# A feed-forward kernel's second product: T1 before the context's B22, the norm's scale row in PSUM, statistics right behind a tile's last part, and B12 before T2 in step one

## The chip, the cores and the metric

The kernel runs on one core of one Trainium2 chip. The metric is the time of one execution in microseconds on the device, as the median of the runs on record.

## What is computed

One layer of a bidirectional hybrid backbone, for 128 context tokens and 1,024 latent tokens of width 1,024. The change touches its last part alone, the second half of the squared-ReLU MLP with its residual and layer norm:

```python
def layer_norm(x, g=None, b=None):
    mu = jnp.mean(xf, -1, keepdims=True)
    var = jnp.mean(jnp.square(xf - mu), -1, keepdims=True)
    y = (xf - mu) * lax.rsqrt(var + LN_EPS)
    y = y * g + b
...
hid = jnp.square(jax.nn.relu(u @ lw['w_fc'] + lw['b_fc']))
x = layer_norm(ALPHA * x + gate2 * (hid @ lw['w_proj'] + lw['b_proj']), lw['ln_g'][1], lw['ln_b'][1])
```

`hid` has 4,096 columns, `w_proj` is 4,096 by 1,024, all in float32; `gate2` is a row of 1,024, one for the context and one for the latents.

## The kernel before

Function `ffn2` computes `hid @ w_proj` in four steps of 1,024 rows of `w_proj` each (`F2`). Every operand is split into a high half, a copy that ScalarE rounds (`hi`, or `w[..., 0]`), and a low half, the rest, subtracted on VectorE or GpSimd (`lo`, `w[..., 1]`; all these have line L68, the copies L67). A product is then three matmuls: high by high, high by low, low by high (`mm3`, lines L111 to L113).

**Products of a step.** The eight weight row blocks of a step come in four pairs; each pair gives the blocks B11, B12 (left and right 512 columns of the first row block), B21 and B22 (of the second). The latents use a seven-product scheme: hidden-layer sums stored in DRAM beforehand (`h_d`) times B11, B21, T2, T3, T4, T1 and B22. T2, T3 and T4 are differences of the blocks that `source` makes just before they are split: VectorE subtracts twice a pair for T2 (L1446, L1447, the second into `tb`), GpSimd once for T3 (L1449) and once for T4 (L1451). T1's block is the first difference of T2, left in place. The 128 context tokens use the four plain blocks with their own hidden layer (`hc_d`). One product for the latents is four blocks `j` of 128 tokens with 12 matmuls of 512 columns each; one for the context is 12 matmuls.

**Order.** `KINDS` (and `KINDS0` in step one) lists the products. For each, `block` runs the four `j`, adds the PSUM bank into the float32 accumulators `C` on VectorE (L1553, L1555), and, for the plain blocks, `context` adds the context's share (L1535). Weights are prepared by a generator, `ahead`, which the loop advances twice a block with `step_work`: it loads raw weights (`load_raw`, L1437) and hidden-layer units (`f2_load`, L1364 and L1367) on SP's queue, and emits splits. At most five half-weights may be prepared ahead of use (`tiles`); they sit in a ring of four buffers and one more. `until` drives the generator until a product's weights have been emitted. All engines run their instructions in the order in which they were emitted, SP's queue of transfers too.

**Ending of step four.** Accumulator tiles are tokens: tile 0 is the context, tiles 1 to 8 are latents, of which 1 to 4 take their right half from B22 and 5 to 8 theirs from T1. `finish` adds the bank to the accumulator, multiplies by the gate and adds the residual with a running sum (L1592, L1593, L1576: three vector operations); `later` does the gate product of tiles 0 to 4's left half on GpSimd (L1585). `norm` is a generator: mean (L1600), ScalarE's Square with its sum (L1601) and root (L1602), then VectorE's reciprocal (L1604); ScalarE's Identity scales and shifts (L1612); the product with the row `lng` and the sum with `lnb` (L1615, L1616) are GpSimd's, or half VectorE's where `how` is 1. Where `how` is 2, VectorE does all in four operations (L1607, L1608). `pump` advances each started norm by one part after each block. B22's context product comes first, then T1's four blocks, then B22's.

Of the kernel before, what the change touches and what calls it, by code (L numbers as in the profile page):

```python
# [12 lines left out]
OP = mybir.AluOpType  # L13
# [26 lines left out]
class Kern:  # L40
# [1306 lines left out]
    KINDS = ["B11", "B12", "B21", "T2", "T3", "T4", "T1", "B22"]  # L1347
    KINDS0 = ["B11", "B21", "T2", "B12", "T3", "T4", "T1", "B22"]
    ROW = {"B11": 0, "T1": 4, "T2": 5, "T3": 2, "B21": 1, "T4": 3, "B22": 6}
# [64 lines left out]
    def ffn2(self, st):  # L1414
# [15 lines left out]
        NB = len(self.F2)  # L1430
        raws = {}

# [5 lines left out]

        def source(b, kind, k):
            f1, f2 = raws[b, k, 0], raws.get((b, k, 1))  # L1440
            b11, b12 = f1[:, 0:512], f1[:, 512:D]
            if kind in ("B11", "B12"):
                return b11 if kind == "B11" else b12
            b21, b22 = f2[:, 0:512], f2[:, 512:D]
            if kind == "T2":
                v.tensor_tensor(b11, b12, b11, OP.subtract)  # L1446
                v.tensor_tensor(t2[k], b22, b11, OP.subtract)  # L1447
            elif kind == "T3":
                g_.tensor_tensor(b12, b22, b12, OP.subtract)  # L1449
            elif kind == "T4":  # L1450
                g_.tensor_tensor(t2[k], b21, t2[k], OP.subtract)  # L1451
            if kind in ("T2", "T4"):
                return t2[k]
            return {"T3": b12, "T1": b11, "B22": b22, "B21": b21}[kind]
# [5 lines left out]
        def ahead():  # L1460

            self.f2_load(0, None)
            for i in range(2):
                load_raw(0, i)
            yield
            for b in range(NB):
# [5 lines left out]
                for kind in self.KINDS if b else self.KINDS0:  # L1472
                    if (b, kind) in done:
                        continue
                    if b == 0 and kind == "T2":
                        for i in range(2):
                            self.f2_split(b, None, i)
                        done.add((b, "ctx"))
# [3 lines left out]
                    if n is not None:  # L1482
                        while 7 * b + n >= 3 and 7 * b + n - 3 not in used:
                            yield
                        self.f2_load(b, n)
                        split += [lambda i=i, n=n: self.f2_split(b, n, i, g_ if i else v) for i in range(2)]
                    for i in range(2):
# [8 lines left out]
                        yield  # L1496
                    done.add((b, kind))

        work = ahead()
# [56 lines left out]

        rows, xh, tails, outs = {}, {}, [], []
        tile_of = lambda t: ctx if t == 0 else Cj[(t - 1) % 4][:, 2 * ((t - 1) // 4):2 * ((t - 1) // 4) + 2].rearrange("p a n -> p (a n)")
        hs = [slice(0, 512), slice(512, D)]
        xq = [(t, n) for ts, n in (((1, 2, 3, 4, 0), 0), ((5, 6, 7, 8), 0), ((0, 5, 6, 7, 8, 1, 2, 3, 4), 1)) for t in ts]  # L1560

# [34 lines left out]
        def norm(t, how=0):  # L1596
# [8 lines left out]
            if how == 2:  # L1605
                for s in hs:
                    v.scalar_tensor_tensor(y[:, s], y[:, s], q(2), rows["lng"][:, s], OP.add, OP.mult)  # L1607
                    v.scalar_tensor_tensor(y[:, s], y[:, s], q(6), rows["lnb"][:, s], OP.mult, OP.add)  # L1608
                    nc.scalar.dma_start(O["y"][t][:, s], y[:, s])
                return  # L1610
            v.tensor_scalar(q(7), q(2), q(6), None, op0=OP.mult)
            nc.scalar.activation(y, y, AF.Identity, scale=q(6), bias=q(7))  # L1612
            yield
            for s, e in zip(hs, (v, g_)) if how else [(slice(0, D), g_)]:
                e.tensor_tensor(y[:, s], y[:, s], rows["lng"][:, s], OP.mult)  # L1615
                e.tensor_tensor(y[:, s], y[:, s], rows["lnb"][:, s], OP.add)  # L1616
            outs.append(lambda: nc.sync.dma_start(O["y"][t], y))

        def pump():
            for x in tails[:]:  # L1620
                if next(x, tails) is tails:
                    tails.remove(x)
            while outs and not xq:
                outs.pop(0)()
# [3 lines left out]
        sb = [big("S") for _ in range(2)]  # L1628
        tails.append(self.store(15, self.H15, [sb[0][:, 0:512], sb[0][:, 512:D], sb[1][:, 0:512]]))
        for b in range(NB):  # L1630
# [4 lines left out]
            for kind in (self.KINDS if b else self.KINDS0)[:6 if last else 8]:  # L1635
                until(b, kind)
                if kind != "B12":
                    for j in range(4):
# [3 lines left out]
                        else:  # L1642
                            block(b, kind, j)
                        if b or kind != "B11":
                            step_work(2)
# [20 lines left out]

        until(b, "B22")
        row("lng", tb[:, 0, 0:D], I["ln_g"][1:2, :])
        row("lnb", tb[:, 1, 0:D], I["ln_b"][1:2, :])
        context(b, "B22", True)  # L1670
        pump()
        finish(0, 1, cx[1])
        tmp, junk = bank("cx", 2), big("junk")
        tails.append(norm(0))
        for j in range(4):
            ps = banks["C", j] = bank()
            product(b, "T1", j, ps, True)
            finish(5 + j, 1, ps, tmp)
            pump()
            tails.append(norm(5 + j))  # L1680
        for j in range(4):
            product(b, "B22", j, banks["C", j], False)
            finish(1 + j, 1, banks["C", j])
            pump()
            tails.append(norm(1 + j, min(j, 2)))
        while tails or outs:
            pump()
# [79 lines left out]
```

## Time and profile before

| | us |
|---|---|
| median of three runs (2229.61 to 2234.83) | 2231.91 |
| profiled execution: time of the run | 2234.51 |
| profiled execution: span | 2232.4 |
| TensorE busy, 12,507 matmuls | 2112.8 (95%) |
| VectorE busy | 1409.6 (63%) |
| ScalarE busy | 994.9 (45%) |
| GpSimd busy | 854.0 (38%) |
| first and last matmul of the second product | 1822.9 and 2203.7 |

PE is TensorE, DVE VectorE, ACT ScalarE, POOL GpSimd; SPq and ACTq are queues of transfers. Matmuls overlap in their pipeline, so a share of 95% says that TensorE rarely stands, not that it runs at its peak. A busy share is a mean over stages of different limits: what counts in one stage is read from windows of that stage. The mean granted clock of TensorE over the span is 0.981 of 2.4 GHz.

### The profile page before, as it was taken

The numbers are of one execution on the slowest core, as the hardware profiler recorded it, in microseconds if no ns is written. First come the engines' busy times: TensorE is split into PE (matmuls) and PEld (weight loads), VectorE is DVE, ScalarE is ACT, GpSimd is POOL, SyncE is SP. The second block draws the span as 40 slices with busy tenths as digits, with TensorE's granted clock in tenths as the row PEclk, the third lists the DMA queues.
The fourth block names the chain that finished last, engine by engine and source line by source line (L and its number), as shares of the span: only waits on it lengthen the run. The fifth ranks groups of instructions, "written<-read, shape, count | busy, mean of one in ns | idle before, by whom it ended". The sixth has DMA issues, their size and how long they took to land. (4 is left out here: it accounts for less than half of the span.)

```text
span 2232.4 us, 31968 instructions
## 1 busy us (share of the span) xinstructions
PE 2112.8 (95%) x12507; PEld 1986.1 (89%) x12507; DVE 1409.6 (63%) x2248; ACT 994.9 (45%) x1634; POOL 854.0 (38%) x507
## 2 busy tenths in 40 slices
PE   7999999999999999999989999999999998999984
PEld 3889999999999989999989998899999996888863
DVE  4456776676675644888564656866454556566677
ACT  5455425414424525777721423655444443343333
POOL 1402213312421312332212214448566656466476
PEclk9999999999999999999989999999999999999997
DMA  7121241142122141110533333454343464342532
GB/s 275 38 71 50 66 146 64 54 133 86 62 87 83 53 77 46 48 48 29 165 120 128 118 117 115 131 199 136 125 143 121 147 245 158 136 170 79 204 118 108
DMA packets 116647, 251.13 MB, mean 112 GB/s; under 512 B 21332, under 2 KB 53716, under 8 KB 111888
## 3 DMA queue, kind: packets, MB, share of 16 engines
q1 hardware_dynamic: 94976, 231.19, 30.7%
q10 hardware_dynamic: 21520, 17.90, 2.4%
q8 instruction: 98, 1.61, 0.3%
q14 instruction: 53, 0.43, 0.1%
HBM read 186.38 MB, written 62.67 MB: 112 GB/s over the span
## 5 line engine op out<-in xcount | busy, mean ns | idle before, releaser
L111 PE MATMUL pj<-hi,w 128*128 128x384 f32 (+1 forms) x2144 | 712.8, 332 | 18.1 <-ACT XP L805 7.9
L112 PE MATMUL pj<-lo,w 128*128 128x384 f32 (+1 forms) x2144 | 709.8, 331 | 12.9 <-DVE lo L68 6.3
L113 PE MATMUL pj<-hi,w 128*128 128x384 f32 (+1 forms) x2144 | 709.2, 331 | 1.3 <-POOL w L68 1.1
L111 PEld LDWEIGHTS pj<-hi,w 128*128 128x128 f32 x2144 | 406.4, 190 | 20.3 <-ACT XP L805 8.2
L112 PEld LDWEIGHTS pj<-lo,w 128*128 128x128 f32 x2144 | 406.4, 190 | 15.4 <-DVE lo L68 6.9
L113 PEld LDWEIGHTS pj<-hi,w 128*128 128x128 f32 x2144 | 406.0, 189 | 1.9 <-POOL w L68 1.4
L68 POOL TENSOR_TENSOR w<-ws,w 128x512 fp32r<-128x512 f32 (+1 forms) x64 | 113.1, 1769 | 292.0 <-ACT w L67 283.8
L111 PE MATMUL pps<-w,hi 128*128 128x512 f32 x512 | 204.0, 398 | 11.3 <-ACT w L67 9.1
L112 PE MATMUL pps<-w,hi 128*128 128x512 f32 x512 | 204.0, 398 | 6.2 <-POOL w L68 4.1
L113 PE MATMUL pps<-w,lo 128*128 128x512 f32 x512 | 202.9, 396 | 1.4 <-DVE lo L68 1.4
L68 DVE TENSOR_TENSOR w<-ws,w 128x1024 fp32r<-128x1024 f32 (+1 forms) x85 | 112.7, 1334 | 122.6 <-ACT w L67 122.5
L67 ACT ACTIVATE w<-ws 128x1024 fp32r<-128x1024 f32 (+1 forms) x149 | 129.5, 878 | 80.8 <-PE pj L113 67.5
L467 POOL PARTITION_ALL_REDUCE aacc<-aacc x16 | 56.0, 3541 | 256.6 <-DVE aacc L466 256.6
L722 POOL TENSOR_TENSOR CS<-Cst,CS 128x516 fp32r<-128x516 f32 x56 | 73.8, 1319 | 158.2 <-ACT CS L721 147.7
L111 PE MATMUL pj<-Th,w 128*128 128x288 f32 x416 | 123.3, 296 | 8.0 <-ACT e L1297 8.0
L111 PEld LDWEIGHTS pps<-w,hi 128*128 128x128 f32 x512 | 98.0, 191 | 34.5 <-ACT w L67 10.4
L112 PEld LDWEIGHTS pps<-w,hi 128*128 128x128 f32 x512 | 98.0, 191 | 29.7 <-POOL w L68 4.9
L113 PE MATMUL pj<-Th,w 128*128 128x288 f32 x416 | 122.6, 295 | 0.0
L112 PE MATMUL pj<-Tl,w 128*128 128x288 f32 x416 | 122.5, 295 | 0.0
L113 PEld LDWEIGHTS pps<-w,lo 128*128 128x128 f32 x512 | 98.1, 192 | 23.4 <-DVE lo L68 1.9
L68 POOL TENSOR_TENSOR lo<-lo,hi 128x1024 fp32r<-128x1024 f32 (+1 forms) x31 | 84.8, 2735 | 74.0 <-ACT hi L67 74.0
L67 ACT ACTIVATE w<-raw 128x512 fp32r<-128x512 f32 x88 | 50.9, 622 | 109.9 <-issue 62.8
(348 smaller groups left out, 4493.2 us busy)
## 6 DMA issues: line engine op xcount, KB each, us to landing
ws<-in_w_in SPq DMA_DIRECT2D x56, 512.0 KB
lo<-h_d SPq DMA_DIRECT2D x28, 1024.0 KB
aw<-in_w_ada SPq DMA_DIRECT2D x64, 256.0 KB
ws<-in_w_fc SPq DMA_DIRECT2D x32, 512.0 KB
h_d<-Hf SPq DMA_DIRECT2D x32, 512.0 KB
raw<-in_w_pr SPq DMA_DIRECT2D x32, 512.0 KB
h_d<-S SPq DMA_DIRECT2D x48, 256.0 KB
gm<-gs ACTq DMA_DIRECT2D x48, 192.0 KB
```

Of the source, the lines that this page charges most:

```text
L67: self.nc.scalar.activation(hi, x, AF.Copy)
L68: (eng or self.nc.vector).tensor_tensor(lo, x, hi.bitcast(F), OP.subtract)
L111: mm(out, lhsT=ah, rhs=bh, start=first, stop=False, skip_group_check=onto)
L112: mm(out, lhsT=ah, rhs=bl, start=False, stop=False, skip_group_check=onto)
L113: mm(out, lhsT=al, rhs=bh, start=False, stop=last, skip_group_check=onto)
L467: nc.gpsimd.partition_all_reduce(acc[j], acc[j], channels=128, reduce_op=ReduceOp.add)
L722: nc.gpsimd.tensor_tensor(CS[d][1], Cst[d], CS[d][0].bitcast(F), OP.subtract)
```

## The change

- In the last step T1's four blocks come before the context's B22, and each is followed by that tile's mean, Square and root at once (`start`) and by two steps of the weight generator. The residual loads are reordered to match.
- The norm's scale row is copied into two PSUM banks (`lng`), and VectorE's intermediate result `u` lies in PSUM too, so that each of its scaling operations has one large operand there. The context's norm is VectorE's (`how` 2), tiles 2 and 3 are halved between GpSimd and VectorE. VectorE's tiles are stored by SP's queue, no longer ScalarE's.
- In steps two to four T2's and T3's subtractions are emitted right behind B12's and B21's weights (`raw_done`).
- In step one B12 comes before T2, T2's hidden-layer unit is loaded ahead of the second row blocks' weights, these are loaded in halves, the right ones first, and the sums of the last hidden rows (`last_sums`) start after T3's first block instead of at once.

```diff
-    KINDS0 = ["B11", "B21", "T2", "B12", "T3", "T4", "T1", "B22"]
+    KINDS0 = ["B11", "B21", "B12", "T2", "T3", "T4", "T1", "B22"]
...
         def source(b, kind, k):
+            if (b, kind, k) in raw_done:
+                return raw_done.pop((b, kind, k))
...
             self.f2_load(0, None)
-            for i in range(2):
-                load_raw(0, i)
+            load_raw(0, 0)
+            self.f2_load(0, 2)
+            for s in (slice(512, D), slice(0, 512)):
+                for k in range(4):
+                    if s.start:
+                        raws[0, k, 1] = big("raw")
+                    nc.sync.dma_start(raws[0, k, 1][:, s], I["w_pr"][2 * k + 1][:, s])
             yield
...
                     done.add((b, kind))
+                    if b and kind in ("B12", "B21"):
+                        x = {"B12": "T2", "B21": "T3"}[kind]
+                        for k in range(4):
+                            raw_done[b, x, k] = source(b, x, k)
+                            if k % 2:
+                                yield
...
             if how == 2:
-                for s in hs:
-                    v.scalar_tensor_tensor(y[:, s], y[:, s], q(2), rows["lng"][:, s], OP.add, OP.mult)
-                    v.scalar_tensor_tensor(y[:, s], y[:, s], q(6), rows["lnb"][:, s], OP.mult, OP.add)
-                    nc.scalar.dma_start(O["y"][t][:, s], y[:, s])
+                for s, g in zip(hs, lng):
+                    v.scalar_tensor_tensor(u, y[:, s], q(2), g, OP.add, OP.mult)
+                    v.scalar_tensor_tensor(y[:, s], u, q(6), rows["lnb"][:, s], OP.mult, OP.add)
+                    nc.sync.dma_start(O["y"][t][:, s], y[:, s])
                 return
...
-            for s, e in zip(hs, (v, g_)) if how else [(slice(0, D), g_)]:
-                e.tensor_tensor(y[:, s], y[:, s], rows["lng"][:, s], OP.mult)
-                e.tensor_tensor(y[:, s], y[:, s], rows["lnb"][:, s], OP.add)
+            if how:
+                v.tensor_tensor(u, y[:, hs[1]], lng[1], OP.mult)
+                v.tensor_tensor(y[:, hs[1]], u, rows["lnb"][:, hs[1]], OP.add)
+            s = hs[0] if how else slice(0, D)
+            g_.tensor_tensor(y[:, s], y[:, s], rows["lng"][:, s], OP.mult)
+            g_.tensor_tensor(y[:, s], y[:, s], rows["lnb"][:, s], OP.add)
...
-        until(b, "B22")
+        until(b, "T1")
...
-        context(b, "B22", True)
-        pump()
-        finish(0, 1, cx[1])
         tmp, junk = bank("cx", 2), big("junk")
-        tails.append(norm(0))
+
+        def start(x):
+            new.append(x)
+            next(x)
+
         for j in range(4):
             ps = banks["C", j] = bank()
             product(b, "T1", j, ps, True)
             finish(5 + j, 1, ps, tmp)
+            start(norm(5 + j))
+            step_work(2)
             pump()
-            tails.append(norm(5 + j))
+        until(b, "B22")
+
+        lng = [bank(), bank()]
+        for o, s in zip(lng, hs):
+            nc.scalar.activation(o, rows["lng"][:, s], AF.Copy)
+        context(b, "B22", True)
+        pump()
+        finish(0, 1, cx[1])
+        u = bank("cx", 2)
+        start(norm(0, 2))
         for j in range(4):
             product(b, "B22", j, banks["C", j], False)
             finish(1 + j, 1, banks["C", j])
+            start(norm(1 + j, (0, 1, 1, 2)[j]))
             pump()
-            tails.append(norm(1 + j, min(j, 2)))
```

VectorE in step one, before, from the first eviction of B21 (`C<-pps,C`) on; `raw` and `tb` rows are T2's subtractions, `ctx` is the context's eviction:

```order
L1555 TENSOR_TENSOR C_17466<-pps,C_17466 128x512
L68 TENSOR_TENSOR lo<-lo,hi 128x512 x2
L1446 TENSOR_TENSOR raw<-raw 128x512
L1447 TENSOR_TENSOR tb<-raw 128x512
L1446 TENSOR_TENSOR raw<-raw 128x512
L1447 TENSOR_TENSOR tb<-raw 128x512
L68 TENSOR_TENSOR w<-tb,w 128x512
L1555 TENSOR_TENSOR C_17467<-pps,C_17467 128x512
L1555 TENSOR_TENSOR C_17468<-pps,C_17468 128x512
L1555 TENSOR_TENSOR C_17469<-pps,C_17469 128x512
L1535 TENSOR_TENSOR ctx<-pps,bp 128x512
L68 TENSOR_TENSOR lo<-lo,hi 128x1024
```

and now (line L1446 is now L1448, L1553 is L1567, L1555 is L1569, L1535 is L1549):

```order
L1569 TENSOR_TENSOR C_17466<-pps,C_17466 128x512
L68 TENSOR_TENSOR lo<-lo,hi 128x512 x2
L68 TENSOR_TENSOR w<-raw,w 128x512
L1569 TENSOR_TENSOR C_17467<-pps,C_17467 128x512
L1569 TENSOR_TENSOR C_17468<-pps,C_17468 128x512
L1569 TENSOR_TENSOR C_17469<-pps,C_17469 128x512
L1549 TENSOR_TENSOR ctx<-pps,bp 128x512
L68 TENSOR_TENSOR w<-raw,w 128x512
L1448 TENSOR_TENSOR raw<-raw 128x512
L1449 TENSOR_TENSOR tb<-raw 128x512
L1448 TENSOR_TENSOR raw<-raw 128x512
L1449 TENSOR_TENSOR tb<-raw 128x512
```

T2's subtractions moved from in front of B21's other three evictions to behind the context's; B12's weights (`w<-raw`) stand before them.

GpSimd in step four, before, from T2's first weight (`w<-tb`) on; `raw<-raw` is T3's subtraction, `C<-C,g2l` a gate product:

```order
L68 TENSOR_TENSOR w<-tb,w 128x512
L68 TENSOR_TENSOR lo<-lo,hi 128x1024
L68 TENSOR_TENSOR w<-tb,w 128x512
L1449 TENSOR_TENSOR raw<-raw 128x512 x2
L1585 TENSOR_TENSOR C_17466<-C_17466,g2l 128x512
L1585 TENSOR_TENSOR C_17467<-C_17467,g2l 128x512
L1585 TENSOR_TENSOR C_17468<-C_17468,g2l 128x512
L68 TENSOR_TENSOR lo<-lo,hi 128x1024
L1585 TENSOR_TENSOR C_17469<-C_17469,g2l 128x512
L1585 TENSOR_TENSOR ctx<-ctx,g2c 128x512
L1449 TENSOR_TENSOR raw<-raw 128x512 x2
L1451 TENSOR_TENSOR tb<-raw,tb 128x512 x2
```

and now:

```order
L1451 TENSOR_TENSOR raw<-raw 128x512 x4
L68 TENSOR_TENSOR w<-tb,w 128x512
L68 TENSOR_TENSOR lo<-lo,hi 128x1024
L1599 TENSOR_TENSOR C_17466<-C_17466,g2l 128x512
L68 TENSOR_TENSOR w<-tb,w 128x512
L1599 TENSOR_TENSOR C_17467<-C_17467,g2l 128x512
L1599 TENSOR_TENSOR C_17468<-C_17468,g2l 128x512
L68 TENSOR_TENSOR lo<-lo,hi 128x1024
L1599 TENSOR_TENSOR C_17469<-C_17469,g2l 128x512
L1599 TENSOR_TENSOR ctx<-ctx,g2c 128x512
L1453 TENSOR_TENSOR tb<-raw,tb 128x512 x2
```

All four of T3's subtractions moved ahead of T2's weights; before, they stood in two pairs, the second behind the gate products.

ScalarE in step four, before, from T1's hidden-layer unit (`hi<-lo`) to the second norm; `w<-raw` are weight copies of T1 and B22, `junk` is Square:

```order
L67 ACTIVATE hi<-lo 128x1024 x2
L67 ACTIVATE w<-raw 128x512 x4
L67 ACTIVATE hi<-lo 128x1024 x2
L67 ACTIVATE w<-raw 128x512 x2
L1601 ACTIVATE junk,sts<-ctx,sts 128x1024
L1602 ACTIVATE sts<-sts,eps 128x1
L1612 ACTIVATE ctx<-ctx,sts 128x1024
L1601 ACTIVATE junk,sts<-C_17466,sts 128x1024
L1602 ACTIVATE sts<-sts,eps 128x1
L1612 ACTIVATE C_17466<-C_17466,sts 128x1024
```

and now:

```order
L67 ACTIVATE hi<-lo 128x1024 x2
L67 ACTIVATE w<-raw 128x512 x4
L1615 ACTIVATE junk,sts<-C_17466,sts 128x1024
L1616 ACTIVATE sts<-sts,eps 128x1
L67 ACTIVATE hi<-lo 128x1024 x2
L1615 ACTIVATE junk,sts<-C_17467,sts 128x1024
L1616 ACTIVATE sts<-sts,eps 128x1
L67 ACTIVATE w<-raw 128x512 x2
L1626 ACTIVATE C_17466<-C_17466,sts 128x1024
L1615 ACTIVATE junk,sts<-C_17468,sts 128x1024
L1616 ACTIVATE sts<-sts,eps 128x1
L1626 ACTIVATE C_17467<-C_17467,sts 128x1024
```

B22's hidden-layer unit and its last two weight copies now stand behind Square and root of tile 5 and of tile 6.

## Rows read from the trace of the kernel before

**Rows 1.** Windows of the second product: busy (starts), granted clock, DMA share, GB/s

```profile
1840.00:1880.00 40.00, 33.51 (x123) 25.38 (x122) 23.56 (x27) 13.80 (x20) 22.41 (x13) 0.87 0.39 149
1890.00:1900.00 10.00, 10.00 (x46) 8.28 (x45) 8.24 (x9) 6.72 (x11) 9.96 (x5) 1.00 1.01 413
2000.00:2040.00 40.00, 40.00 (x177) 33.04 (x177) 25.89 (x31) 10.19 (x15) 15.90 (x10) 1.00 0.21 72
2140.00:2150.00 10.00, 7.38 (x23) 5.08 (x22) 5.55 (x10) 4.41 (x6) 8.62 (x7) 0.83 0.37 134
2160.00:2190.00 30.00, 20.16 (x78) 15.66 (x77) 20.45 (x35) 6.44 (x11) 9.87 (x5) 0.83 0.36 123
2204.00:2232.40 28.40, 0.09 (x1) 0.00 (x0) 20.62 (x26) 8.62 (x15) 20.95 (x9) 0.55 0.33 129
```

**Rows 2.** TensorE's waits from 1815 on: total us, times, longest

```profile
PE pps L111 <- ACT w L67: 9.1, 3, 7.0
PE pps L112 <- POOL w L68: 4.1, 2, 2.9
```

**Rows 3.** TensorE's timeline in step one: start, us, line, tiles, idle before

```profile
1833.81 0.39 PE L111 MATMUL pps<-w,hi 128*128 128x512 f32 x1
...
1860.13 0.79 PE L112 MATMUL pps<-w,hi 128*128 128x512 f32 x1 [1.21 <-POOL w L68]
```

**Rows 4.** TensorE's timeline at the context's B22, and its last matmul

```profile
2166.85 0.39 PE L111 MATMUL pps<-w,hi 128*128 128x512 f32 x1
...
2175.36 0.79 PE L111 MATMUL pps<-w,hi 128*128 128x512 f32 x1 [6.96 <-ACT w L67]
...
2179.03 0.79 PE L112 MATMUL pps<-w,hi 128*128 128x512 f32 x1 [2.88 <-POOL w L68]
...
2203.70 0.39 PE L113 MATMUL pps<-w,lo 128*128 128x512 f32 x1
```

**Rows 5.** VectorE's timeline in step one, same columns

```profile
1839.21 0.68 DVE L1446 TENSOR_TENSOR raw<-raw 128x512 f32<-128x512 f32 x1
...
1854.47 0.69 DVE L1535 TENSOR_TENSOR ctx<-pps,bp 128x512 f32<-128x512 f32 x1 [4.79 <-PE pps L113]
```

**Rows 6.** GpSimd's timeline in step four, around T2 and T3

```profile
2115.80 1.66 POOL L68 TENSOR_TENSOR w<-tb,w 128x512 fp32r<-128x512 f32 x1 [2.70 <-ACT w L67]
...
2128.68 5.16 POOL L1585 TENSOR_TENSOR C<-C,g2l 128x512 f32<-128x512 f32 x3
...
2140.54 2.51 POOL L1449 TENSOR_TENSOR raw<-raw 128x512 f32<-128x512 f32 x2
```

**Rows 7.** GpSimd's timeline, its first scaling of an output tile

```profile
2191.65 2.41 POOL L1615 TENSOR_TENSOR ctx<-ctx,tb 128x1024 f32<-128x1024 f32 x1 [12.67 <-ACT ctx L1612]
```

**Rows 8.** VectorE's timeline in the ending

```profile
2170.36 0.69 DVE L1576 SCALAR_TENSOR_TENSOR C<-xb,pps 128x512 f32<-128x512 f32 x1
...
2203.07 0.69 DVE L1592 TENSOR_TENSOR pps<-pps,C 128x512 f32<-128x512 f32 x1
...
2214.24 2.75 DVE L1607 SCALAR_TENSOR_TENSOR C<-C,sts,tb 128x512 f32<-128x512 f32 x1
...
2228.47 0.75 DVE L1608 SCALAR_TENSOR_TENSOR C<-C,sts,tb 128x512 f32<-128x512 f32 x1
```

**Rows 9.** ScalarE's timeline at the last B22 and in the ending

```profile
2172.78 2.00 ACT L67 ACTIVATE hi<-lo 128x1024 fp32r<-128x1024 f32 x2 [10.93 <-DMA lo<-h_d]
...
2174.69 1.13 ACT L67 ACTIVATE w<-raw 128x512 fp32r<-128x512 f32 x2
...
2204.22 1.13 ACT L1601 ACTIVATE junk<-C,sts 128x1024 f32<-128x1024 f32 x1
...
2205.48 0.29 ACT L1602 ACTIVATE sts<-sts,eps 128x1 f32<-128x1 f32 x1
...
2206.26 1.24 ACT L1612 ACTIVATE C<-C,sts 128x1024 f32<-128x1024 f32 x1 [0.48 <-DVE sts L1611]
```

More of the change, by code (lines that the diff above doesn't have):

```diff
@@ L1430, in ffn2 @@
         NB = len(self.F2)
-        raws = {}
+        raws, raw_done = {}, {}
         def load_raw(b, i):
@@ L1474, in ahead @@
                         continue
-                    if b == 0 and kind == "T2":
+                    if b == 0 and kind == "B12":
                         for i in range(2):
@@ L1484, in ahead @@
                             yield
-                        self.f2_load(b, n)
+                        if (b, n) != (0, 2):
+                            self.f2_load(b, n)
                         split += [lambda i=i, n=n: self.f2_split(b, n, i, g_ if i else v) for i in range(2)]
@@ L1555, in block @@
                 v.tensor_tensor(o, ps, o, OP.add)
-        rows, xh, tails, outs = {}, {}, [], []
+        rows, xh, tails, outs, new = {}, {}, [], [], []
         tile_of = lambda t: ctx if t == 0 else Cj[(t - 1) % 4][:, 2 * ((t - 1) // 4):2 * ((t - 1) // 4) + 2].rearrange("p a n -> p (a n)")
         hs = [slice(0, 512), slice(512, D)]
-        xq = [(t, n) for ts, n in (((1, 2, 3, 4, 0), 0), ((5, 6, 7, 8), 0), ((0, 5, 6, 7, 8, 1, 2, 3, 4), 1)) for t in ts]
+        xq = [(t, n) for ts, n in (((1, 2, 3, 4, 0), 0), ((5, 6, 7, 8), 0), ((5, 6, 7, 8, 0, 1, 2, 3, 4), 1)) for t in ts]
         def row(n, o, src):
@@ L1613, in norm @@
             yield
-            for s, e in zip(hs, (v, g_)) if how else [(slice(0, D), g_)]:
-                e.tensor_tensor(y[:, s], y[:, s], rows["lng"][:, s], OP.mult)
-                e.tensor_tensor(y[:, s], y[:, s], rows["lnb"][:, s], OP.add)
+            if how:
[4 more added lines that the diff above has]
+            g_.tensor_tensor(y[:, s], y[:, s], rows["lnb"][:, s], OP.add)
             outs.append(lambda: nc.sync.dma_start(O["y"][t], y))
         def pump():
-            for x in tails[:]:
+            old = tails[:]
+            tails.extend(new)
+            new.clear()
+            for x in old:
                 if next(x, tails) is tails:
@@ L1628, in ffn2 @@
         sb = [big("S") for _ in range(2)]
-        tails.append(self.store(15, self.H15, [sb[0][:, 0:512], sb[0][:, 512:D], sb[1][:, 0:512]]))
+        last_sums = (self.store(15, self.H15, [sb[0][:, 0:512], sb[0][:, 512:D], sb[1][:, 0:512]]))
         for b in range(NB):
@@ L1643, in ffn2 @@
                             block(b, kind, j)
+                        if b == 0 and kind == "T3" and j == 0:
+                            tails.append(last_sums)
                         if b or kind != "B11":
@@ L1683, in ffn2 @@
             finish(1 + j, 1, banks["C", j])
+            start(norm(1 + j, (0, 1, 1, 2)[j]))
             pump()
-            tails.append(norm(1 + j, min(j, 2)))
-        while tails or outs:
+        while new or tails or outs:
             pump()
```

## Prediction, made before the changed kernel ran

> **What bounds the kernel now.** I read the windows of the second product first, then TensorE's waits, then the timelines of single engines at the places that these name.
>
> In full windows TensorE starts 177 matmuls in 40 us, one every 0.226 us, and three stretches fall short of it [rows 1]. Step one, 1840 to 1880, has 123 of 177. The ten microseconds from 2140 have 23 of 44. From 2160 to 2190 there are 78 of 133. That is 12, 5 and 12 us lost. Behind the last matmul come 28.4 us with one record of TensorE in them. In these some 58 us something other than TensorE sets the pace; elsewhere nothing counts that only makes another engine faster. The granted clock is 0.83 to 0.87 in the three, so part of the loss is time at the lower of its two levels, 1.2 GHz, behind a wait.
>
> What ends the waits is weight preparation: ScalarE's copy 9.1 us, GpSimd's low half 4.1 us [rows 2]. The longest is at the context's B22: its first half starts at 2166.85, its second half stands still to 2175.36 and again to 2179.03; the last matmul of all starts at 2203.70 [rows 4].
>
> Behind that, GpSimd and VectorE scale the output tiles. A full tile costs GpSimd two operations of 2.41 us [rows 7]. A VectorE operation with its large inputs in SBUF takes 2.75 us while GpSimd works and 0.75 us when it has stopped; one with an operand in PSUM takes 0.69 us with GpSimd busy beside it [rows 8].
>
> **The ending: T1 ahead of B22, statistics at once, scale row in PSUM.** I walk it on the clock of the old profile, with T4's matmuls done at 2166.85 as they were. T1's now follow at once: T1's weights were ready by then, since ScalarE's next copies, from 2172.78, are B22's [rows 9]. Its 48 matmuls last to 2177.7; the first half of the context's B22 ends at 2179.1.
>
> B22's second half now queues behind the norms of tiles 5 and 6. T4's last vector work is done at 2171.05 [rows 8]. Tile 5's finish (three operations of 0.69 with gaps, 2.2) ends at 2173.3, its mean at 2173.5. ScalarE squares and takes the root in 1.55 us, as from 2204.22 to 2205.77 in the old rows [rows 9], so to 2175.1. Then come B22's two high halves, 2.00, to 2177.1; their load, for which they waited till 2172.78 before [rows 9], is in. VectorE's low half waits for the first of these and takes about 1.2 (estimate: twice a 512-wide operation), to 2177.3; tile 6's finish and mean follow, to 2179.7; ScalarE's square and root to 2181.3; the two weight copies, 1.13 [rows 9], to 2182.5. GpSimd takes the first at 2181.9 and needs 1.3 (half of 2.41, and a little), so the second half of the context runs at 2183.3, after a wait of 4.2 us. The 100 matmuls behind 2179.03 took 24.7 us instead of 22.6 [rows 4], 2.1 of it the lower clock; with the same here, the 52 that remain end near 2197, 6 us ahead of before.
>
> The end itself hangs on GpSimd. Tile 5's Identity follows the weight copies and two small vector operations, 0.49 between the old root and Identity [rows 9]: behind VectorE's weight at 2183.2 that is 2183.7, plus 1.24, so the first scaling starts at 2185.0; the old one started at 2191.65 [rows 7]. GpSimd does tiles 5 to 8 and 1 whole, ten operations of 2.42, and the lower halves of tiles 2 and 3, four of 1.21 (half of a whole one) to 1.72 (beside VectorE [rows 6]). VectorE works with PSUM operands there, so I take 1.35: 24.2 + 5.4 = 29.6, to 2214.6. Supply doesn't break: a tile costs ScalarE 1.55 + 1.24 = 2.8 [rows 9], GpSimd 4.8. From the last vector operation's end, 2229.22, to the span's end are 3.2 us for a 256 KB store [rows 8]; 512 KB add 0.6 at the 413 GB/s of [rows 1]. The end is 2218.4, against 2232.4: **14.0 less**.
>
> VectorE's own share ends no later. With the scale row in PSUM its halves cost 0.7 instead of 2.7. From the context's last matmul, near 2185.5, it has five finishes (11.5), the context's and tile 4's four operations each (6), two half tiles (3.8) and small ones: 23, and some 5 us of waiting for ScalarE. That is 2213.5, and a 256 KB store ends at 2216.7.
>
> Of no price of their own: the two copies of the scale row into PSUM (0.6 each) lie in the 2 us a tile that ScalarE has over GpSimd; the reordered x loads keep their places in SP's queue; the stores that leave ScalarE's queue for SP's stand among other stores.
>
> **Step four's T3: subtractions ahead.** GpSimd's T3 subtractions stood behind the gate products, 5.16 us for three, so the second pair came at 2140.54 while TensorE waited [rows 6]. Now all four stand in front of T2's first low half. T2 has room: GpSimd did its first piece at 2115.80 [rows 6], and T2's matmuls began near 2129 (2166.85 less 144 matmuls and the 5 us lost), 13 us later; four subtractions cost 5.2. Of 4.8 us lost I keep 0.4: **4.4 less** (bounds 0 and 4.8). In steps two and three nothing waited, and the 13 us cover the 5.2.
>
> **Step one: B12 ahead of T2.** T2's subtractions stood between evictions on VectorE from 1839.21 [rows 5], and T2's second weight held TensorE up to 1860.13 [rows 3]. They now stand behind the eviction of the context's first half, which needs both context products: B21 starts at 1833.81 [rows 3], 48 + 24 matmuls bring 1850.1, the eviction (at 1854.47 before [rows 5]) ends at 1851.0, B12's vector weight at 1851.7. B12's 12 matmuls run unhindered to 1852.8. T2's first sources end at 1854.5, the weight copies at 1855.0, the first high half at 1856.0: TensorE idles 3.2. The second sources want VectorE from 1857.2, while GpSimd does T2's low half (2.41) till 1859.5. By the 0.68 us that such an operation took with GpSimd idle [rows 5], the second weight would be whole at 1861.2. But the 2.75 against 0.75 above says that it waits for the one on GpSimd: 2.1 more, so 1863.3. Against these 3.2 us later than 1860.13 stand 12 matmuls already done (2.7): **+0.5**, with bounds of -10 (T2 ready when TensorE is) and +4.
>
> The Trainium skill (SBUF — State Buffer, "SBUF: two separate sides") calls it an exclusive lock: a GpSimd operation and a VectorE one with two SBUF inputs take turns, whole instructions at a time. The trace agrees in the 2.75 against 0.75; by the rule the second weight comes at 1863.3, by durations with GpSimd idle the change would be 2.1 us better.
>
> **Sum.** -14.0 - 4.4 + 0.5 = -17.9. The profiled execution took 2234.51 us with a span of 2232.4; the median of the three runs, 2231.91, lies 2.6 lower. So I expect 2214.0 as the median, 2216.6 for a run like the profiled one.
>
> **Rivals.**
> - *B22 later still.* The nine links from 2171.05 to 2183.3 take half as long again, 6 us, for instance by x loads that arrive late for tiles 5 and 6. For it: in the old chain each engine waited for the one before, and a link's delay goes on in full. Against it: no link is over 2.2 us, and each has its row. It takes 6 from the 14.0: 2220.
> - *Step one freed as well.* If T2 is ready when TensorE is, 10 us more go: 2204. For it: T2's load leaves earlier, ahead of half the weights. Against it: in the walk T2 waits for VectorE, not for its load.
> - *The subtractions choke VectorE (slower).* From step two on T2's eight stand in a block, ahead of evictions and beside T3's four on GpSimd: 5.5 us alone, 22 if each waits 2.75. Over the 13 us of room that is 9 a step in three steps, 27 - 17.9: 2241. It decides from 20.5 us a block on, since 7.5 a step are needed to undo the gain and 4.5 more. Against it: every one of the eight would have to meet a busy GpSimd.
> - *The ending moves but doesn't shorten.* If statistics or stores set it, the wait would return behind the last matmul, and T3's 4.4 less 0.5 alone remain: 2228. Against it: GpSimd's scalings and VectorE's 2.75 us operations fill the old ending.
>
> **Chances.** Forecast 0.73 (2208 to 2220), B22 later 0.12, step one freed 0.08, no shorter ending 0.04, choked 0.03. The range 2206 to 2222 holds nearly all of the forecast and most of the second. Within 0.2%, 4.5 us, about what a measurement of this kernel can tell from no change, lie the fourth rival and a little of the second: 0.05; slower 0.03; faster 0.92.
>
> **What would show it.** Right: TensorE passes from T4 to T1 without a wait, then waits 3 to 5 us within the context's B22; GpSimd's scalings run without a gap for some 30 us and the last store follows them; VectorE's scalings take 0.7; no loss at step four's T3; in step one a wait of the old size, at T2, from 1853 and again to 1863. Wrong: a wait at T1, GpSimd starved between scalings, waits at T2 of later steps, or a T2 that starts at 1853.

## The result, and the profile after

The changed kernel took 2217.66 us (median of four runs, 2217.04 to 2220.55) against 2232.59 for the kernel before (four runs, 2229.61 to 2234.83): a ratio of 0.9935, 95% interval 0.9919 to 0.9950. It is faster by 14.9 us, within the predicted range, 3.7 us above the predicted time.

The same windows as [rows 1], with the two of the ending moved to where it now lies:

```profile
1840.00:1880.00 40.00, 32.72 (x128) 25.34 (x127) 22.03 (x26) 13.15 (x18) 19.90 (x13) 0.87 0.30 101
2140.00:2150.00 10.00, 9.26 (x42) 7.22 (x41) 8.35 (x13) 2.64 (x3) 5.28 (x4) 1.00 0.80 270
2163.00:2193.00 30.00, 26.32 (x102) 20.89 (x101) 22.52 (x51) 16.30 (x26) 14.09 (x7) 0.89 0.46 150
2195.00:2215.80 20.80, 0.23 (x2) 0.00 (x0) 14.21 (x31) 8.16 (x12) 16.34 (x9) 0.61 0.45 177
```

Step one still has only 128 matmul starts of 177. At T3 of step four 42 of 44 are back, and of the thirty microseconds behind T4 102 of 133. Behind the last matmul (2194.84) 21.0 us are left, 28.7 before.

TensorE's waits from 1815 on, as [rows 2]:

```profile
PE pps L111 <- ACT w L67: 6.1, 2, 3.1
PE pps L111 <- ACT hi L67: 2.9, 1, 2.9
PE pps L112 <- POOL w L68: 2.4, 5, 0.9
```

Waits for ScalarE's weight copies are down from 9.1 to 6.1 us, those for GpSimd from 4.1 to 2.4; the one for a high half is new. TensorE's timeline says where: step one's T2, T3 of step four, then the matmuls that follow T4's last, as [rows 3, 4]:

```profile
1855.94 0.50 PE L111 MATMUL pps<-w,hi 128*128 128x512 f32 x1 [2.86 <-ACT hi L67]
...
1861.44 0.79 PE L111 MATMUL pps<-w,hi 128*128 128x512 f32 x1 [2.98 <-ACT w L67]
1863.14 0.80 PE L112 MATMUL pps<-w,hi 128*128 128x512 f32 x1 [0.92 <-POOL w L68]
...
2143.04 0.50 PE L112 MATMUL pps<-w,hi 128*128 128x512 f32 x1 [0.74 <-DVE w L68]
...
2163.44 0.39 PE L111 MATMUL pps<-w,hi 128*128 128x512 f32 x1
...
2178.99 0.79 PE L111 MATMUL pps<-w,hi 128*128 128x512 f32 x1 [3.12 <-ACT w L67]
2180.34 0.80 PE L112 MATMUL pps<-w,hi 128*128 128x512 f32 x1 [0.56 <-POOL w L68]
...
2194.84 0.39 PE L113 MATMUL pps<-w,lo 128*128 128x512 f32 x1
```

T2's second weight holds TensorE to 1863.14. At T3 a wait of 0.74 us is left. T4 is over at 2163.44, the start of the next matmul (all times "behind T4" below count from this start). T1 runs with no wait, and the context's B22 waits for ScalarE's weight copy until 2178.99 and for GpSimd until 2180.34. VectorE's timeline, a subtraction of step one and its last scaling, as [rows 5, 8]:

```profile
1857.06 2.85 DVE L1448 TENSOR_TENSOR raw<-raw 128x512 f32<-128x512 f32 x1
...
2210.49 0.75 DVE L1622 SCALAR_TENSOR_TENSOR C<-pps,sts,tb 128x512 f32<-128x512 f32 x1
```
GpSimd's timeline, first and last scaling, as [rows 7]:

```profile
2182.50 2.38 POOL L1632 TENSOR_TENSOR C<-C,tb 128x1024 f32<-128x1024 f32 x1 [2.22 <-ACT C L1626]
...
2210.39 1.26 POOL L1633 TENSOR_TENSOR C<-C,tb 128x512 f32<-128x512 f32 x1
```

GpSimd's fourteen scalings run without a gap worth naming from 2182.50 to 2211.65; VectorE's last ends 0.4 us earlier, at 2211.24. Both fill the ending. ScalarE's timeline ahead of the first scaling, as [rows 9]:

```profile
2170.71 1.16 ACT L1615 ACTIVATE junk<-C,sts 128x1024 f32<-128x1024 f32 x1 [12.53 <-DVE sts L1614]
...
2172.19 1.99 ACT L67 ACTIVATE hi<-lo 128x1024 fp32r<-128x1024 f32 x2
2176.85 1.15 ACT L1615 ACTIVATE junk<-C,sts 128x1024 f32<-128x1024 f32 x1 [2.67 <-DVE sts L1614]
...
2178.32 1.13 ACT L67 ACTIVATE w<-raw 128x512 fp32r<-128x512 f32 x2
2181.19 1.24 ACT L1626 ACTIVATE C<-C,sts 128x1024 f32<-128x1024 f32 x1 [1.73 <-DVE sts L1625]
```

Read it downwards: tile 5's Square, B22's high halves, tile 6's Square, B22's weight copies, then tile 5's Identity. The idle time in brackets is ScalarE's, each time until VectorE had finished a tile or made its factors.

### The profile page after: what moved, and what is told of

Read it like the earlier page. It is cut to its first block, busy times and chain, and to the rows that moved or that the text cites. A ratio compares the mean times of both kernels' runs of the same rounds, so it can differ in the third digit from the quotient of the medians.

```text
span 2215.8 us, 32002 instructions
## 1 busy us (share of the span) xinstructions
PE 2109.8 (95%) x12507; PEld 1983.8 (90%) x12507; DVE 1416.0 (64%) x2250; ACT 994.6 (45%) x1636; POOL 849.4 (38%) x507
## 5 line engine op out<-in xcount | busy, mean ns | idle before, releaser
L112 PE MATMUL pj<-lo,w 128*128 128x384 f32 (+1 forms) x2144 | 709.8, 331 | 13.2 <-DVE lo L68 6.3
L113 PEld LDWEIGHTS pps<-w,lo 128*128 128x128 f32 x512 | 97.4, 190 | 22.2 <-DVE lo L68 1.0
L1569 DVE TENSOR_TENSOR C<-pps,C 128x512 f32<-128x512 f32 x84 | 57.0, 686 | 67.8 <-PE pps L113 67.8
```

Source lines behind the costliest of these rows:

```text
L112: mm(out, lhsT=ah, rhs=bl, start=False, stop=False, skip_group_check=onto)
L113: mm(out, lhsT=al, rhs=bh, start=False, stop=last, skip_group_check=onto)
L1569: v.tensor_tensor(o, ps, o, OP.add)
```

## The experiments

Each ratio is to runs of before on the same chip (medians 2233.5 to 2235.2 in these). Single runs of one kernel differ by up to 10.6 us, and the profiles show where most of that comes from: the first matmul of step one started between 1820.56 and 1828.37 us in them, though no edit touches anything ahead of it. So the table has, beside the times, three stretches of each profile, all read from TensorE's timeline: T3 and T4 of step four (T3's first matmul to the start that follows T4's last; 21.8 at full pace), the ending (from that start to the span's end), and the whole from step one's first matmul to the end. From T1's second block in step one to T3 of step four all fourteen profiles need 238.8 us. Each stretch is from one execution; in three kernels whose ending has the same code and whose T3 took the same time (changed, old_step_one, step_one_t2) the ending is 52.1 to 52.4 us, so differences under 0.3 us say nothing.

| kernel | T3, T4 | ending | whole | median, us | ratio to before, interval |
|---|---|---|---|---|---|
| before | 27.1 | 65.6 | 409.5 | 2232.6 | |
| changed | 23.6 | 52.4 | 392.9 | 2217.7 | 0.9935 (0.9919 to 0.9950) |
| old_ending | 23.6 | 64.5 | 405.0 | 2232.2 | 0.9984 (0.9975 to 0.9993) |
| no_t3_ahead | 22.2 | 51.5 | 390.7 | 2216.7 | 0.9919 (0.9905 to 0.9932) |
| no_ahead | 28.2 | 50.1 | 395.3 | 2221.3 | 0.9942 (0.9930 to 0.9953) |
| old_step_one | 23.6 | 52.4 | 392.8 | 2219.0 | 0.9927 (0.9914 to 0.9940) |
| b22_first | 23.6 | 50.7 | 391.2 | 2217.6 | 0.9920 (0.9906 to 0.9933) |
| order_alone | 22.3 | 60.2 | 399.4 | 2227.2 | 0.9962 (0.9950 to 0.9974) |
| sbuf_row | 23.6 | 56.4 | 396.9 | 2223.2 | 0.9945 (0.9932 to 0.9957) |
| late_mean | 23.6 | 49.4 | 389.9 | 2215.6 | 0.9918 (0.9905 to 0.9931) |
| late_mean_t1 | 23.6 | 48.0 | 388.6 | 2214.6 | 0.9920 (0.9907 to 0.9933) |
| step_one_t2 | 23.6 | 52.1 | 392.9 | 2218.0 | 0.9929 (0.9917 to 0.9941) |
| lighter_pool | 22.2 | 50.2 | 389.4 | 2213.8 | 0.9920 (0.9905 to 0.9934) |
| two_undone | 22.2 | 49.7 | 388.9 | 2212.7 | 0.9902 (0.9885 to 0.9918) |

The theory was the prediction's: the ending carries 14 us, T3's early subtractions 4, step one nothing. The rivals are in the expectations.

**old_ending.** The last stage of step four and `norm` as in the kernel before, cut:

```diff
-        until(b, "T1")
+        until(b, "B22")
...
+        context(b, "B22", True)
+        pump()
+        finish(0, 1, cx[1])
...
-            start(norm(5 + j))
-            step_work(2)
             pump()
+            tails.append(norm(5 + j))
...
-                for s, g in zip(hs, lng):
+                for s in hs:
```

> The changed kernel with the ending of before put back (context's B22 ahead of T1, mean and Square a tile later, the scale row read from SBUF, stores as before); step one and the early subtractions stay as changed. Theory, that the ending carries the gain: the two profiles give the ending 65.6 us behind T4's last matmul before and 52.4 after, so 13.2 us come back, about 2230.9 us, ratio to before 0.998 to 0.999. Rival, that the gain came from the first half of step four and the new ending only moved its waits: under 4 us come back, about 2221 us.

The whole is 12.1 us longer than the changed kernel's, so 4.5 of the 16.6 us remain, T3's 3.5 among them. The ending carries most of the gain.

**no_t3_ahead** and **no_ahead.**

```diff
-                    if b and kind in ("B12", "B21"):
+                    if b and kind == "B12":
```

and, for the second,

```diff
-                    if b and kind in ("B12", "B21"):
+                    if False:
```

> The changed kernel with T3's GpSimd subtractions back at their old place in steps two to four, right ahead of T3's first weights; T2's stay early. Theory, that T3's stall in step four was these subtractions and that the ending passes on what comes ahead of it: 3.4 us come back (T4's last matmul stood 3.4 us earlier in the profile of after), about 2221 us. Rival, that the ending, bound by VectorE and GpSimd, swallows a delay ahead of it: within 1 us of the changed kernel's 2217.7.

> The changed kernel with both sets of early subtractions, T2's on VectorE and T3's on GpSimd, back at their old places in steps two to four; step one and the ending stay as changed. T3's four groups and the waits in them took 27.1 us before, 23.6 in the changed kernel, 22.2 with T2's subtractions alone early. Theory, that T2's early subtractions give all of the gain at T3 and T3's own cost 1.4 to 2 of it: T3's stage returns to 27.1 us and the time is 3.5 us over the changed kernel and 5 over the one with T2's alone, about 2221 us (ratio to before 0.994 to 0.995). Rival, that the new ending swallows a delay ahead of it: within 1 us of the changed kernel.

Without T3's early subtractions nothing comes back: the stretch is 1.4 us shorter still and the ending 0.9, so the theory falls. The median lies within the rival's 1 us, but there was no delay for the ending to swallow, so the run doesn't test the rival. Without T2's as well the stretch is 28.2. So the gain at T3 is T2's, though T2 itself never waited in step four. TensorE's waits at T3 in the kernel before:

```profile
2142.54 0.50 PE L111 MATMUL pps<-w,hi 128*128 128x512 f32 x1 [1.28 <-ACT w L67]
2143.66 0.51 PE L112 MATMUL pps<-w,hi 128*128 128x512 f32 x1 [0.62 <-DVE w L68]
...
2145.34 0.66 PE L112 MATMUL pps<-w,hi 128*128 128x512 f32 x1 [0.73 <-DVE w L68]
```
And in no_ahead:

```profile
2142.81 0.50 PE L111 MATMUL pps<-w,hi 128*128 128x512 f32 x1 [1.28 <-ACT w L67]
2143.93 0.50 PE L112 MATMUL pps<-w,hi 128*128 128x512 f32 x1 [0.62 <-DVE w L68]
...
2145.61 0.79 PE L112 MATMUL pps<-w,hi 128*128 128x512 f32 x1 [0.52 <-DVE w L68]
```

The waits are nearly the same. That no_ahead needs 28.2 and not 27.1 fits TensorE's clock behind them: from 2145 to 2150 the granted clock is 0.50 there, its lower level, and 0.66 in the kernel before. In no_ahead the ending did swallow part of a delay: the stretch is 4.6 us longer than in the changed kernel, the whole 2.4.

GpSimd's timeline says how T2's subtractions help T3, here of no_t3_ahead:

```profile
2117.72 1.74 POOL L68 TENSOR_TENSOR w<-tb,w 128x512 fp32r<-128x512 f32 x1
...
2134.77 3.01 POOL L1451 TENSOR_TENSOR raw<-raw 128x512 f32<-128x512 f32 x2
```
The first of these in the kernel before, in the timeline of [rows 6]:

```profile
2124.11 1.66 POOL L68 TENSOR_TENSOR w<-tb,w 128x512 fp32r<-128x512 f32 x1 [2.10 <-ACT w L67]
```

GpSimd's low half of T2's second weight starts 6.4 us earlier (0.5 of it because step one began so much earlier in that run), since ScalarE need no longer wait for VectorE's subtractions. What stands behind it on GpSimd, the gate products and T3's second pair, moves up nearly as much: 2134.77 against 2140.54. T3's own early block leads to a race between the low halves of T2's hidden-layer unit, one on VectorE, one on GpSimd, which VectorE mostly loses. The two timelines in the changed kernel:

```profile
2121.32 2.39 POOL L68 TENSOR_TENSOR lo<-lo,hi 128x1024 fp32r<-128x1024 f32 x1
2121.34 3.45 DVE L68 TENSOR_TENSOR lo<-lo,hi 128x1024 fp32r<-128x1024 f32 x1
...
2140.12 2.87 DVE L68 TENSOR_TENSOR w<-raw,w 128x512 fp32r<-128x512 f32 x2
```

VectorE's low half of T2's unit, 1.2 us where it comes first, took 3.45 beside GpSimd's, VectorE didn't catch up, and T3's second low halves, whose copies were there at 2128.7, began at 2140.12; T3 waits 0.7 us for them. In all eight profiles that read 23.6 GpSimd's low half began 0.02 us ahead of VectorE's and VectorE's took 3.44 to 3.46; order_alone, with the same instructions here, has 22.3, and in it VectorE got ahead, though its record begins 0.01 us later, and GpSimd's took 3.48:

```profile
2119.33 3.48 POOL L68 TENSOR_TENSOR lo<-lo,hi 128x1024 fp32r<-128x1024 f32 x1
2119.34 1.22 DVE L68 TENSOR_TENSOR lo<-lo,hi 128x1024 fp32r<-128x1024 f32 x1
```

So the 1.4 us look like the price not of the subtractions but of which engine's low half goes first; the one profile in which VectorE's did is the evidence.

T3's subtractions early without T2's weren't tried: they overwrite a block that T2's read.

**old_step_one** and **step_one_t2.** The first puts back the order, the loads and the place of `last_sums`:

```diff
-    KINDS0 = ["B11", "B21", "B12", "T2", "T3", "T4", "T1", "B22"]
+    KINDS0 = ["B11", "B21", "T2", "B12", "T3", "T4", "T1", "B22"]
...
-            load_raw(0, 0)
-            self.f2_load(0, 2)
...
+            for i in range(2):
+                load_raw(0, i)
```

The second:

```diff
                         done.add((b, "ctx"))
+                        for k in range(4):
+                            raw_done[b, "T2", k] = source(b, "T2", k)
+                            if k % 2:
+                                yield
```

> The changed kernel with step one of before: T2 ahead of B12, its loads whole and in the old order, the last sums of the first product at their old place. Theory, that step one's stall was only moved (T3 of step one starts at 1875.0 us in both profiles): within 1 us of the changed kernel, 2216.7 to 2218.7. Rival, that the new order saves something that comes out only later, in B12's and T3's weights or in step two: 4 to 10 us more, 2222 to 2228.

> The changed kernel with T2's eight subtractions of step one issued ahead of B12's weights (right behind the split of the context's unit) in place of behind them. Theory, that step one's stall at T2 is a matter of these subtractions' place on VectorE: their eight times 0.69 us fit its 8.8 us of idle time between 1840 and 1850 us, TensorE's 3.3 us ahead of T2 and its 5 us of waits and lower clock in T2's first tile go, and 2 to 3 us of it come back at T3, whose weights GpSimd makes: about 2211.5 us (2210 to 2214). Rival, that T3's and T4's weights hang on GpSimd's own chain, which starts no earlier: all of it comes back, within 1 us of 2217.7.

From step one's first matmul to its T1's second block are 78.07 us before, 78.17 changed, 78.07 put back, 78.40 with T2 early: three orders, almost one length. old_step_one's median lies 0.3 us outside the theory's band, its whole 0.1 from the changed kernel's. In the last the stall has only moved a third time. TensorE's timeline:

```profile
1845.30 0.79 PE L111 MATMUL pps<-w,hi 128*128 128x512 f32 x1 [3.83 <-DVE C L1573]
...
1863.74 0.50 PE L113 MATMUL pps<-w,lo 128*128 128x512 f32 x1 [2.70 <-DVE lo L68]
```

VectorE's subtractions hold up its evictions, so TensorE waits for a bank in B21; T2's unit is still late, as the low halves ahead of its own took 2.79 and 1.77 us beside GpSimd. The rival's size was right (all comes back). Its reason is not shown: the runs don't tell whether GpSimd's chain for T3 and T4 alone sets the 78.

**order_alone** and **sbuf_row.** The first is old_ending with the context's B22 (and its x load) moved behind T1's blocks:

```diff
-        context(b, "B22", True)
-        pump()
-        finish(0, 1, cx[1])
...
             tails.append(norm(5 + j))
+        context(b, "B22", True)
+        pump()
+        finish(0, 1, cx[1])
```

The second:

```diff
-                for s, g in zip(hs, lng):
+                for s, g in zip(hs, [rows["lng"][:, s] for s in hs]):
...
-                v.tensor_tensor(u, y[:, hs[1]], lng[1], OP.mult)
+                v.tensor_tensor(u, y[:, hs[1]], rows["lng"][:, hs[1]], OP.mult)
...
-        for o, s in zip(lng, hs):
-            nc.scalar.activation(o, rows["lng"][:, s], AF.Copy)
```

> The changed kernel with the ending of before, in which only T1's four tiles stand ahead of the context's B22 (B22's preparation ahead of both, mean and Square a tile later, the scale row in SBUF, stores as before). Theory, that the order only takes TensorE's wait away and that VectorE's and GpSimd's row of norms decides: TensorE's last matmul comes some 10 us earlier, but the time gains 3 to 7 of the ending's 13 us, about 2225 us. Rival, that the order is the whole ending: about 2218 us. Second rival, that without the other parts it gives nothing: about 2231 us.

> The changed kernel with the norm's scale row left in SBUF and the two copies to PSUM dropped; all else as changed. Theory, that VectorE's scalings with two operands in SBUF wait for GpSimd: its six first operations on half a tile take 2.0 to 2.8 us in place of 0.69 to 0.76, and as VectorE works without a break from 2181 to 2211 us the end moves by most of 6 x 1.7 = 10 us, 2224 to 2228 us. Rival, that GpSimd's row of scalings is the only bound and VectorE's waits fall beside it: under 2 us, about 2219.

The order alone is worth 4.4 us of the ending (64.5 to 60.2), though TensorE's last matmul now starts 24.3 us behind T4 instead of 35.8: the theory held, TensorE's waits are not all that counts here. The row is worth 4.0, not 6 to 10: between theory and rival. VectorE's timeline in sbuf_row:

```profile
2198.61 2.47 DVE L1621 SCALAR_TENSOR_TENSOR pps<-ctx,sts,tb 128x512 f32<-128x512 f32 x1
2201.11 0.75 DVE L1622 SCALAR_TENSOR_TENSOR ctx<-pps,sts,tb 128x512 f32<-128x512 f32 x1
```
And in order_alone, where the intermediate result is in SBUF too:

```profile
2199.68 2.71 DVE L1630 TENSOR_TENSOR C<-C,tb 128x512 f32<-128x512 f32 x1
...
2202.39 2.75 DVE L1621 SCALAR_TENSOR_TENSOR C<-C,sts,tb 128x512 f32<-128x512 f32 x1
2205.17 2.71 DVE L1622 SCALAR_TENSOR_TENSOR C<-C,sts,tb 128x512 f32<-128x512 f32 x1
```

An operation with the row in SBUF takes 2.47 us beside a busy GpSimd, the next, which reads `u` from PSUM, 0.75. Not all six such operations were held up: the last three took 0.70 to 0.91. In order_alone operations of both kinds are held up. GpSimd pays as well, where the two meet, in its timeline of sbuf_row:

```profile
2200.48 2.79 POOL L1632 TENSOR_TENSOR C<-C,tb 128x1024 f32<-128x1024 f32 x1
```

2.79 for the usual 2.35. What else the new ending holds (`u` in PSUM, the context's tile on VectorE, the stores) was not run apart. If the parts add, it is worth between 6 and 7 us: the ending fell by about 12, of which the order gave 4.4 and the row 4.0, while the statistics, below, cost 2.9.

**late_mean**, **late_mean_t1** and **b22_first.**

```diff
-            start(norm(5 + j))
             step_work(2)
             pump()
+            tails.append(norm(5 + j))
```

That is late_mean_t1; late_mean does the same for the context and B22's tiles. b22_first keeps `start`:

```diff
-        until(b, "T1")
+        until(b, "B22")
...
-            step_work(2)
             pump()
-        until(b, "B22")
```

> The changed kernel with mean and Square of a tile issued one tile later, as before, in place of right behind the tile's last part. Theory, that they open the chain to GpSimd's first scaling: it starts one tile of T1, 2.7 us, later and all scalings with it, about 2220.5 us (2219.5 to 2222). Rival, that B22's copies, which then stand ahead of the Squares on ScalarE, take the wait out of the context's B22 and the two cancel: within 1 us of 2217.7.

> The changed kernel with mean and Square a tile later for T1's four tiles alone; for the context and B22's four tiles they stay right behind the last part. All of them late gave 2215.6 us, 0.9918 of before, and an ending 2.9 us shorter in the profile. Theory, that the harm was only where B22's copies stand behind T1's Squares on ScalarE: the ending stays 3 us shorter than the changed kernel's, and the last tiles' early Squares take off up to 1 us more, 2214 to 2215.5. Rival, that VectorE's small operations right behind each last part also hold up B22's tiles: 2216 to 2218.

> The changed kernel with all of B22's preparation (the unit's split and the second weights) issued ahead of T1's first tile, as it was before, and the rest of the new ending kept. Theory, that the last 0.9 us and the wait in the context's B22 come from B22's copies standing behind a tile's mean, Square and root on ScalarE and VectorE: TensorE's 4.2 us of waits there go, VectorE's idle time of 2.6 and 2.7 us between tiles 5 and 7 goes too, GpSimd's first scaling starts 3 to 5 us earlier, about 2213.5 us (2212 to 2215). Rival one, that the end hangs on VectorE's and GpSimd's unbroken work from 2181 us on and the wait was cover: within 1 us of 2217.7. Rival two, that the unit's split, put ahead of tile 5's Square in ScalarE's order, holds the Square up: 1 to 3 us slower, about 2220.

In the profiles, statistics at once cost time: without them the ending is 2.9 us shorter, and 4.4 if only T1's come late. The ratios point the same way, but their intervals overlap the changed kernel's. Both theory and rival of late_mean were wrong in sign or size; what the rival named, B22's copies ahead of the Squares, outweighs the later Squares. late_mean_t1's theory held (2214.6). ScalarE's timeline in late_mean, against the rows of after above:

```profile
2169.14 1.14 ACT L67 ACTIVATE w<-raw 128x512 fp32r<-128x512 f32 x2
2173.24 1.16 ACT L1615 ACTIVATE junk<-C,sts 128x1024 f32<-128x1024 f32 x1 [2.97 <-DVE sts L1614]
```
And GpSimd's:

```profile
2176.96 2.40 POOL L1632 TENSOR_TENSOR C<-C,tb 128x1024 f32<-128x1024 f32 x1 [2.72 <-ACT C L1626]
```

T4 is over at 2162.16 here. The weight copies come 7.0 us behind it, not 14.9, TensorE never waits, and the first scaling starts 14.8 us behind it, not 19.1. In the changed kernel VectorE waits 2.59 and 2.67 us for B22's copies, which stand behind Squares on ScalarE. Tile 6's finish and tile 5's reciprocal stand behind these waits.

b22_first took TensorE's waits away as well (its last matmul is 7.1 us nearer to T4's), and gained 1.7 us in the profile, nothing in the median (2217.6 for 2217.7): most of TensorE's wait in the context's B22 cost nothing, as rival one says, and rival two's reason is there too. All of B22's low halves then stand ahead of tile 5's finish. ScalarE's timeline:

```profile
2171.82 2.01 ACT L67 ACTIVATE hi<-lo 128x1024 fp32r<-128x1024 f32 x2 [10.35 <-DMA lo<-h_d]
...
2179.30 1.16 ACT L1615 ACTIVATE junk<-C,sts 128x1024 f32<-128x1024 f32 x1 [4.43 <-DVE sts L1614]
```

The high halves wait for their load, VectorE behind them, and tile 5's Square comes 12.6 us behind T4 (2166.73), in late_mean 11.1. In the changed kernel it came 7.3 us behind, earliest of the three, and yet its first scaling came latest (19.1; 17.7 in b22_first, 14.8 in late_mean).

**lighter_pool** and **two_undone.** Both have T3's subtractions and T1's statistics back at their old places; lighter_pool differs from two_undone in one line, marked + here:

```diff
-            tails.append(norm(5 + j))
+            tails.append(norm(5 + j, j // 2))
```

> Three edits together on the changed kernel, for a version faster than both: T3's subtractions back at their old place, mean and Square a tile later for T1's tiles, and tiles 7 and 8 scaled half on VectorE (from the PSUM row), half on GpSimd, so that GpSimd has 10 halves in place of 12. Theory, that GpSimd's unbroken row of scalings, 29.2 us, is the bound of the ending once its first one is early: 2 x 2.5 us leave it and come back in part as VectorE's 2 x 1.45 us, so 1.4 us from T3, 3 from the copies and 2 to 4 from the row, about 2210 us (2208.5 to 2212), 0.988 to 0.990 of before. Rival, that VectorE, which ends within 0.5 us of GpSimd in the changed kernel, is the bound: no better than late_mean's 2215.6, or worse by 1 to 3 us.

> The changed kernel with the two parts of the change undone that cost time in the runs so far, and with GpSimd's 12 halves kept: T3's subtractions at their old place (1.4 us at T3) and mean and Square a tile later for T1's tiles (4.3 us of the ending). Theory, that the two add up: from the first matmul of step one to the end 387 us in the profile, against 392.9 in the changed kernel; about 2213 us (2211 to 2215), 0.990 to 0.992 of before. Rival, that T4's earlier end is lost in the ending again, as VectorE is behind with T4's tiles by the same amount: 388.5 us in the profile, no better than late_mean_t1's 2214.6.

GpSimd with two halves fewer stands still for 4.51 us: it waits for tile 1's Identity, whose factors stand behind VectorE's longer queue. Its timeline of lighter_pool:

```profile
2196.09 2.35 POOL L1632 TENSOR_TENSOR C<-C,tb 128x1024 f32<-128x1024 f32 x1 [4.51 <-ACT C L1626]
```
VectorE's in the same kernel, a split ahead of T1's first finish and the last scaling:

```profile
2168.28 1.23 DVE L68 TENSOR_TENSOR lo<-lo,hi 128x1024 fp32r<-128x1024 f32 x1 [0.67 <-ACT hi L67]
...
2206.70 0.75 DVE L1622 SCALAR_TENSOR_TENSOR C<-pps,sts,tb 128x512 f32<-128x512 f32 x1
```

The rival held: the ending is 50.2 us, worse than late_mean_t1's 48.0, and the ratio is no better than late_mean's (0.9920 for 0.9918). Of the two splits twelve halves on GpSimd and six on VectorE are the better. two_undone has the lowest ratio of all, 0.9902 of before. Its interval lies just below the changed kernel's, but overlaps those of late_mean, late_mean_t1 and lighter_pool; its profile (388.9 us) is no better than late_mean_t1's, and two rows of GpSimd's and VectorE's timelines say why:

```profile
2168.89 2.42 POOL L68 TENSOR_TENSOR lo<-lo,hi 128x1024 fp32r<-128x1024 f32 x1 [7.16 <-ACT hi L67]
2169.02 3.37 DVE L68 TENSOR_TENSOR lo<-lo,hi 128x1024 fp32r<-128x1024 f32 x1
```

The low half that took 1.23 us in lighter_pool takes 3.37: GpSimd's began at 2168.89, 0.13 us earlier. Its median fits the theory, its profile the rival. Whether T3's 1.4 us reach the end stays open: they did between the profiles of the changed kernel and no_t3_ahead (392.9 to 390.7), not between those of late_mean_t1 and two_undone.

## Why the prediction was right, and which step failed

- **Ending, -14.0.** 13.2 between the profiles, 12.1 by putting it back. The walk held at its main links: TensorE's wait 3.7 us (4.2 predicted), first scaling 19.1 us behind T4 (18.2; VectorE's T4 backlog ended 0.7 later), scalings 29.2 (29.6), store 4.1 (3.8). What it missed is inside: statistics at once, which it counted as part of the gain and didn't price apart, cost 2.9 to 4.4 in the profiles, and VectorE is as much the bound as GpSimd (lighter_pool). Its 3.8 for VectorE's two half tiles should be 2.8 by its own 0.7 an operation (the trace has 2.8); nothing hangs on it.
- **T3, -4.4.** This step failed. The size was near (3.5), by luck, the mechanism not: it put the gain down to T3's subtractions in front of the gate products. Beside T2's these gave nothing, and seem to have cost 1.4 by a lost race in eight of nine profiles. T2's early subtractions, to which it gave no price, gave 4.9 against before (27.1 to 22.2) and 6.0 against no_ahead (28.2), because GpSimd's whole queue hung on T2's second weight. Of the loss, 1.8 us stayed (23.6 for 21.8) where the prediction left 0.4.
- **Step one, +0.5.** 0.1. T2 started at 1855.94 (1856.0 predicted), its second weight was whole at 1863.14 (1863.3), with the 2.85 us of VectorE's wait for GpSimd in it. By the Trainium skill (SBUF — State Buffer, "SBUF: two separate sides") a VectorE operation with two inputs in SBUF and a GpSimd operation take turns by whole instructions. The trace agrees in the 2.85 beside 0.68, and in sbuf_row, where an operation with one input in PSUM takes 0.75 behind one of 2.47.
- **Sum.** -16.6 in the profiles (2232.4 to 2215.8) for -17.9. The other 2.4 of the 3.7 us are the step from profile to median: the prediction took off 2.6, as the profiled run of before lay above its median; that of after, 2217.56, lay on it.
- **Rivals.** None came: B22 was not later than walked (a wait of 3.7 us), VectorE didn't choke in steps two to four, T2 wasn't on time, and the ending was shorter.

## What to carry to other kernels

Ask of each early instruction what stands behind it in its queue: T2's subtractions, put early, helped the next product, T3, by way of GpSimd's queue, and Squares put early held up copies that VectorE and TensorE needed next. Removing a wait of the busiest engine is worth little where its results queue for others: 7 us less on TensorE gave 1.7 in the profile. Compare stretches of the profiles, from a common matmul, when whole runs differ by more than the effect.

## What the runs showed of the hardware

Where a VectorE and a GpSimd operation meet, which of them comes first can be worth as much as an edit, and it falls out differently in kernels with the same code there. VectorE's low half of B22's hidden-layer unit took 3.37 us in two_undone, where GpSimd's began 0.13 us earlier, and 1.23 in lighter_pool, where VectorE's was first by 0.99; the first scaling then came 16.9 and 14.7 us behind T4. In T2's unit, where the two begin within 0.02 us of each other, VectorE's took 3.45 in the changed kernel and 1.22 in order_alone, and T3 and T4 took 23.6 and 22.3.
